# Split fp32r prompt scores and an order from a simulated timeline, in a hybrid attention layer on one Trainium2 core

## The chip, the cores and the metric

The kernel is one program on one NeuronCore of a Trainium2 chip. The metric is the device time of one execution in microseconds (us); lower is better. A core has a matrix engine (TensorE, PE in the profile, its weight loads PEld), three engines for elementwise work (VectorE or DVE, ScalarE or ACT, GpSimd or POOL), and queues that issue DMA transfers, here nearly all on SyncE (SP). Each engine runs its own list of instructions in order and waits for the others by semaphores. Matrix results go to PSUM, eight banks of 128 x 512 f32, and are copied ("evacuated") from there.

## The reference

One layer serves 512 prompt tokens and 64 sample tokens with model width 1024. What matters here, cut to the core:

```python
h = x + W_out [ GDN(n) ; DiffAttn(n) ]     # n = rmsnorm(x), one input projection for both
h = h + MemCrossAttn(rmsnorm(h))
h = h + W2 relu(W1 rmsnorm(h))^2           # then a final rmsnorm

def one(args):                             # differential attention: 4 heads, two halves c of 64 each
    s = jnp.einsum('bqhcd,bkhcd->bhcqk', qi, kf) * scale
    s = jnp.where(visible, s, -jnp.inf)    # whole chunks of 64 keys
    p = jax.nn.softmax(s, axis=-1)
    a = p[:, :, 0] - lam * p[:, :, 1]
    return jnp.einsum('bhqk,bkhe->bqhe', a, vf)

# gated delta (GDN), chunks in sequence, 4 heads: a unit triangular system per chunk, then
def step(S, xs):
    vn = u_c - w_c @ S
    o = qg_c @ S + qk_c @ vn
    S = S * gl_c + kd_c.T @ vn
```

All inputs and outputs are float32. Outputs are the two results, the new keys, values and states.

## The kernel before

Activations stand with features on the partitions and the 576 tokens along the free axis; the 512 prompt tokens are four tiles of 128, the sample a fifth tile (index 4). A projection (`project`) multiplies a 128-column weight block with all tokens in two halves of 256 and 320 tokens. Each f32 weight block is loaded into `raw`, split into a high and a low fp32r part (`wh`, `wl`; L161 on ScalarE, L162 on VectorE) and multiplied with split tokens, so 40 matmuls make one block's projection. Its results go to PSUM tiles `pr` (three banks). The other banks are `ba` (two), `g0`, `g1` and `gs` (one each). In the names of instructions below a tile has a number behind it, one for each time it is taken from its pool.

The gated delta works on chunks c of 128 prompt tokens (0 to 3) and one of the sample (4). `gdn_prep(c, ...)` builds a chunk's triangular system and inverts it level by level: bank g0 for even c, g1 for odd c, tiles `At`, `Dt`, `Y`, `B` with the digit c % 2 (one buffer each for At, Dt and Y) and `X`, `KQ`, `vb`, `kd` (two buffers each). One level is two turns of Y (L113), products with B (L107), a copy of X on ScalarE (L763), Y on VectorE (L764), a product with X, and two subtractions on VectorE (L771, L772). `gdn_scan` then steps the state S in bank gs.

The differential attention goes head by head. `diff_project(h)` makes q, k and v of a head. q is evacuated to `qz` (L957 and `add_to`): two copies of 128 rows, one for each half c, with zeros in the rows of the other half, so that one matmul of 128 rows gives one half's scores. Keys stand turned in `kdT`, a region of the pair tile e5 of all four heads, values in `vtm`, the other half of e5. `diff_head(h, between)` then takes the sample's tile and the four prompt tiles: scores in banks g0 and g1 (f32), maximum (L1019), exponentials (L1022), combination (L1026, L1027), turns, product with the values in bank gs. The cross attention and the feed-forward part follow.

No order is written out by hand for these parts. The functions are called in program order, and a list scheduler of the framework sets, when the kernel is built, in which order each engine gets its instructions, within data dependencies and the number of buffers of each tile. Two places are pinned by hand (`in_order`, `issue_after`).

Of the kernel before, what the change touches and what calls it, by code (L numbers as in the profile page):

```python
# [8 lines left out]
F32 = mybir.dt.float32  # L9
F32R = mybir.dt.float32r  # L10
# [27 lines left out]
def hybrid_layer_kernel(  # L38
# [48 lines left out]
    def view(u, i, a, b):  # L87
        return u[:, i].rearrange("p k t -> p (k t)")[:, : a * b].rearrange("p (a b) -> p a b", a=a)
# [104 lines left out]
    def add_to(dst, b, more):  # L193
        A.copy(dst, more)
        V.tensor_tensor(dst, b, dst, ALU.add)
# [734 lines left out]
    nlam = const([P, 1], "nlam")  # L930
    V.scalar_tensor_tensor(nlam, le[:, 1:2], -LAM0, le[:, 0:1], ALU.add, ALU.subtract)

    od, kdT = e3[:, 0], e5[:, 0]
    vtm = view(e5, 1, 4, 4 * P)
    vs = cp.tile([P, 4, P], F32, tag="vs", name="vs")
    cv2 = view(e3, 1, 4, 4 * P).rearrange("p (i b) n -> p i b n", i=2)
    ckT, cvv = cv2[:, 0].rearrange("p b (c n) -> p (b c) n", n=PAST), cv2[:, 1]

    qz = [cp.tile([P, 2, T], F32, tag=f"qz{i}", name=f"qz{i}") for i in range(2)]
    with tc.issue_after(behind_keys[0]), tc.issue_after(behind_keys[1]):  # L940
        for q2 in qz:
            G.memset(q2[64:, 0, :], 0.0)
            G.memset(q2[:64, 1, :], 0.0)
        G.memset(vs[64:], 0.0)

    def diff_project(h):
        hs = slice(h * P, (h + 1) * P)
        for kind, base in (("q", 2056), ("k", 2568), ("v", 3080)):
            def evac(b, a0, n, more):
                ts_ = slice(a0, a0 + n)  # L950
                if kind == "q":
                    for c in range(2):
                        R = slice(64 * c, 64 * c + 64)
                        if more is not None:
                            add_to(qz[h % 2][R, c, ts_], b[R], more[R])
                        else:
                            (A.copy if c else V.tensor_copy)(qz[h % 2][R, c, ts_], b[R])  # L957
                    return
                d = small("zr", [P, 320])[:, :n] if kind == "v" else kdT[:, h, ts_]
                if more is not None:  # L960
                    add_to(d, b, more)
                else:
                    V.tensor_copy(d, b)
                bt = bank()
                for t in range(2):
                    tr(bt[:, t * P : (t + 1) * P], d[:, t * P : (t + 1) * P])
                if a0:
                    tr(bt[:DEC, 256:384], d[:, 256:])
                src, t2 = bt[:, :256].rearrange("p (t d) -> p t d", t=2), slice(a0 // P, a0 // P + 2)
                if kind == "v":  # L970
                    A.copy(vtm[:, t2, hs], src)
# [11 lines left out]
        nc.sync.dma_start(o_dv_p[0, 0, :, h, :].rearrange("(t p) d -> p t d", p=P), vtm[:, :, hs])  # L983
        nc.sync.dma_start(o_dv_s[0, 0, :, h, :], vs[:DEC, h, :])

    def diff_cache():
# [9 lines left out]
    def diff_head(h, between):  # L996


        hs = slice(h * P, (h + 1) * P)
        so, co = tiny([P, 5], "ta"), tiny([P, 5], "ta")  # L1000
        on = small("an", [P, 5, P])
        for t in (4, 0, 1, 2, 3):
            if t == 1:
                between()
            q0 = QT[t][0]
            nk = q0 + P if t < 4 else PAST + DEC
            nb = (nk + P - 1) // P
            pr = []
            mx, l = tiny([P, 2], "ta"), tiny([P, 2], "ta")
            for c in range(2):  # L1010
                b = bank(f"g{c}")
                qq = qz[h % 2][:, c, q0 : q0 + P]
                if t < 4:
                    mm(b[:, :nk], qq, kdT[:, h, :nk])
                    V.memset(b[:64, nk - 64 : nk], -1e30)
                else:
                    mm(b[:, :PAST], qq, ckT[:, h, :])
                    mm(b[:, PAST:nk], qq, kdT[:, h, SEQ:T])
                V.tensor_reduce(mx[:, c : c + 1], b[:, :nk], AX.X, ALU.max)  # L1019
# [3 lines left out]
                pr.append(p)  # L1023
            V.reciprocal(l, l)
            V.tensor_tensor(l[:, 1:2], l[:, 1:2], nlam, ALU.mult)
            V.tensor_scalar(pr[1][:, :nk], pr[1][:, :nk], l[:, 1:2], None, ALU.mult)  # L1026
            V.scalar_tensor_tensor(pr[0][:, :nk], pr[0][:, :nk], l[:, 0:1], pr[1][:, :nk], ALU.mult, ALU.add)  # L1027
            if nk < nb * P:
                G.memset(pr[0][:, nk : nb * P], 0.0)
            bt = bank()  # L1030
            aT = small("aT", [P, 4, P])
            for kb in range(nb):
                tr(bt[:, kb * P : (kb + 1) * P], pr[0][:, kb * P : (kb + 1) * P])
            A.copy(aT[:, :nb, :], v4(bt, nb))
            po = bank("gs")[:, :P]
            for kb in range(nb):
                if t < 4:
                    vv = vtm[:, kb, hs]
# [584 lines left out]
```

## Time and profile before

| | |
|---|---|
| median of 3 runs | 987.23 us (987.15 to 987.32) |
| profiled execution | 987.2 us |
| its span | 985.5 us, mean granted TensorE clock 0.997 |
| instructions | 16923, of them 6403 matmul records on PE |
| DMA traffic | 90.75 MB, mean 92 GB/s |

The span is the time from the first to the last instruction in the trace of one execution; 1.7 us lie around it. Busy shares add up over the span, so an engine can be busy nearly always and still wait at single places. An f32 matmul leaves two records in the trace, an fp32r matmul or a turn (a matmul with the identity, L113) one. L107 and L113 are the lines of the two helpers `mm` and `tr`, through which all matrix work goes, so groups are told apart by their tiles.

### The profile page before, as it was taken

What the parts mean: (1) busy time and instruction counts of PE and PEld (TensorE: products, weight loads), DVE (VectorE), ACT (ScalarE), POOL (GpSimd) and SP (SyncE); (2) the same over time, 40 slices, a digit from 0 to 9 for tenths busy, and PEclk for the clock granted to TensorE, in tenths of its full rate; (3) what the DMA queues carried; (4) which work ended last, traced back from release to release, by engine and by line L of the source; (5) the groups of instructions that cost most, each with busy time, mean ns of one, the idle gap of its engine ahead of it and who ended that gap; (6) DMA issues with size and microseconds to landing.
All of it is one profiled execution on the core that took longest, in us unless ns stands there. A gap on an engine that the chain in (4) does not pass through costs nothing.

```text
span 985.5 us, 16923 instructions
## 1 busy us (share of the span) xinstructions
PE 968.5 (98%) x6403; PEld 891.2 (90%) x6403; DVE 699.7 (71%) x1570; ACT 530.1 (54%) x1194; POOL 58.8 (6%) x127
## 2 busy tenths in 40 slices
PE   9999999999999999999999999999999999999996
PEld 7989899898888878999999999999999999999996
DVE  6666787877676676666557977657867779978674
ACT  7545575344656665444445657665544445555444
POOL 3341011101000000000000000000000000000000
PEclk9999999999999999999999999999999999999998
DMA  7432340103222647333111414222222223223202
GB/s 212 129 119 65 90 138 23 43 23 103 81 68 68 203 131 227 95 94 99 44 44 58 127 54 127 86 86 86 86 87 86 86 86 86 86 86 86 65 23 96
DMA packets 121714, 90.75 MB, mean 92 GB/s; under 512 B 5564, under 2 KB 112206, under 8 KB 121122
## 3 DMA queue, kind: packets, MB, share of 16 engines
q1 hardware_dynamic: 121266, 89.03, 30.9%
q8 instruction: 50, 0.82, 0.3%
q10 hardware_dynamic: 368, 0.66, 0.2%
q14 instruction: 30, 0.25, 0.1%
HBM read 79.93 MB, written 9.75 MB: 91 GB/s over the span
## 4 chain that ended last, share of the span: by engine, by line
PE 83%; DVE 4%; issue 3%; POOL 2%; DMA 2%; ACT 2%; POOLq 0%; ACTq 0%; SPq 0%; DVEq 0%
PE pr L107 51%; PE g L107 12%; PE ba L107 10%; PE gs L107 6%; PE ba L113 3%; PE g L113 1%; POOL tg L208 1%; DMA r<-in_w_ff_dram 1%; DVE p L457 1%; DVE wl L162 0%; DMA grow<-gdram 0%; DMA raw<-in_w_ff_dram 0%; POOL X L607 0%; POOL X L608 0%; DVE on L809 0%
## 5 line engine op out<-in xcount | busy, mean ns | idle before, releaser
L107 PE MATMUL pr<-u,wh 128*128 128x320 f32 (+2 forms) x1240 | 328.7, 343 | 1.3 <-DVE p L323 1.2
L107 PEld LDWEIGHTS pr<-u,wh 128*128 128x128 f32 x1240 | 212.3, 188 | 18.0 <-DVE p L323 1.8
L107 PE MATMUL pr<-u,wl 128*128 128x256 f32 (+1 forms) x816 | 226.7, 302 | 0.0
L107 PEld LDWEIGHTS pr<-u,wl 128*128 128x128 f32 x816 | 149.9, 189 | 2.7 <-DVE wl L388 0.2
L162 DVE TENSOR_TENSOR wl<-raw,wh 128x1024 fp32r<-128x1024 f32 x65 | 79.4, 1223 | 41.3 <-ACT wh L161 41.0
L161 ACT CAST wh<-raw 128x1024 fp32r<-128x1024 f32 x65 | 68.1, 1048 | 65.7 <-PE pr L107 50.5
L107 PE MATMUL pr<-u,w2h 128*128 128x320 f32 (+1 forms) x384 | 98.5, 340 | 0.0
L1369 ACT CAST w2h<-r 128x512 fp32r<-128x512 f32 x56 | 34.7, 620 | 87.9 <-PE pr L107 85.3
L107 PE MATMUL pr<-f,w2h 128*128 128x320 f32 (+1 forms) x288 | 74.3, 340 | 0.1
L107 PEld LDWEIGHTS pr<-u,w2h 128*128 128x128 f32 x384 | 65.0, 188 | 4.5 <-ACT u L1452 0.3
L107 PE MATMUL pr<-u,w2l 128*128 128x256 f32 (+1 forms) x256 | 65.1, 295 | 0.0
L1454 DVE TENSOR_TENSOR u<-u,pr 128x256 f32<-128x256 f32 x96 | 42.3, 448 | 16.9 <-PE pr L107 16.2
L107 PE MATMUL ba<-u,wl 128*128 128x288 f32 x360 | 53.0, 296 | 0.4 <-ACT keep L1405 0.4
L107 PEld LDWEIGHTS pr<-f,w2h 128*128 128x128 f32 x288 | 48.7, 188 | 4.0 <-issue 1.1
L107 PEld LDWEIGHTS ba<-u,wl 128*128 128x128 f32 x360 | 49.2, 188 | 1.2 <-ACT keep L1405 1.1
L107 PE MATMUL pr<-f,w2l 128*128 128x256 f32 (+1 forms) x192 | 48.8, 295 | 0.0
L107 PEld LDWEIGHTS pr<-u,w2l 128*128 128x128 f32 x256 | 46.9, 188 | 1.5
L208 POOL TENSOR_TENSOR tiny<-tiny,nhalf 128x1 f32<-128x1 f32 (+4 forms) x10 | 8.7, 870 | 631.6 <-DVE tiny L1522 529.8
L1370 DVE TENSOR_TENSOR w2l<-r,w2h 128x512 fp32r<-128x512 f32 x56 | 38.5, 688 | 10.7 <-ACT w2h L1369 10.4
L107 PE MATMUL pr<-wh,u 128*128 128x512 f32 x128 | 41.4, 401 | 0.0
L1414 ACT ACTIVATE c<-c 128x288 f32<-128x288 f32 x48 | 20.6, 443 | 29.5 <-DVE c L1413 29.5
L107 PEld LDWEIGHTS pr<-f,w2l 128*128 128x128 f32 x192 | 35.2, 188 | 1.2
(514 smaller groups left out, 2025.1 us busy)
## 6 DMA issues: line engine op xcount, KB each, us to landing
raw<-in_w_ff_dram SPq DMA_DIRECT2D x36, 512.0 KB
raw<-in_w_in_dram SPq DMA_DIRECT2D x28, 512.0 KB
r<-in_w_ff_dram SPq DMA_DIRECT2D x56, 256.0 KB
raw<-in_w_mem_k_dram SPq DMA_DIRECT2D x8, 512.0 KB
raw<-in_w_mem_v_dram SPq DMA_DIRECT2D x8, 512.0 KB
raw<-in_w_out_dram SPq DMA_DIRECT2D x8, 512.0 KB
raw<-in_w_mem_q_dram SPq DMA_DIRECT2D x8, 512.0 KB
raw<-in_w_mem_o_dram SPq DMA_DIRECT2D x8, 512.0 KB
```

The costliest lines, as they stand in the source:

```text
L107: i = nc.tensor.matmul(out, lhsT, rhs, start=start, stop=stop, skip_group_check=skip_group_check)
L113: i = nc.tensor.transpose(out, in_, ident[:n, :n])
L161: A.copy(wh, raw)
L162: V.tensor_tensor(wl, raw, wh.bitcast(F32), ALU.subtract)
L208: G.tensor_tensor(out, in_, bc(nhalf[: in_.shape[0], 0:1], list(in_.shape)), ALU.pow)
L457: V.scalar_tensor_tensor(yv[:, :n], cb[:, i : i + n], cwt[:, m, i : i + 1], yv[:, :n], ALU.mult, ALU.add)
L1369: A.copy(wh, src)
L1370: V.tensor_tensor(wl, src, wh.bitcast(F32), ALU.subtract)
L1414: A.activation(c, c, AF.Relu)
L1454: V.tensor_tensor(am, am, b, ALU.add)
```

## The change

There are two parts. First, the prompt scores. q and k of the prompt are split into a high and a low fp32r part. q's two parts go to tiles in the tags At0 and At1, and four DMAs stack them for each half c: high part in rows 0 to 63, low part in rows 64 to 127 of `qs`. k's parts go to a pair tile `kdu` (two slots, one for even and one for odd heads, in the place of e5); three DMAs repeat each part in both row halves. A half's scores are then two fp32r matmuls into the same bank, one with the high part of k and one with the low part. The sample's q and new keys go to tiles in the tags Y0 and Y1 and stay f32. Values move from e5 to four tiles in the tags kd, vb, X and KQ, and their output goes by four DMAs instead of one. The halves are taken in the order 1, 0.

Second, the scheduler: `schedule_with_timeline_sim=True` has all instructions of the kernel ordered by a simulation of the whole timeline.

```diff
-    od, kdT = e3[:, 0], e5[:, 0]
-    vtm = view(e5, 1, 4, 4 * P)
+    od = e3[:, 0]
+    kdu = pair(5, F32R)
+    vtm = [small(tag, [P, 4 * P]) for tag in ("kd", "vb", "X", "KQ")]
...
-    qz = [cp.tile([P, 2, T], F32, tag=f"qz{i}", name=f"qz{i}") for i in range(2)]
+    qs = [cp.tile([P, 2, T], F32R, tag=f"qz{i}", name=nm("qs")) for i in range(2)]
+    qy = [small(f"Y{i}", [P, 4 * P]) for i in range(2)]
+    qz, knew = [y[:, : 2 * P].rearrange("p (c n) -> p c n", c=2) for y in qy], [y[:, 2 * P : 2 * P + DEC] for y in qy]
...
+        qn = [small(tag, [P, SEQ], dt=F32R) for tag in ("At0", "At1")]
+        kn = kd_of(h)[:, 0]
...
                 if kind == "q":
-                    for c in range(2):
-                        R = slice(64 * c, 64 * c + 64)
-                        if more is not None:
-                            add_to(qz[h % 2][R, c, ts_], b[R], more[R])
-                        else:
-                            (A.copy if c else V.tensor_copy)(qz[h % 2][R, c, ts_], b[R])
+                    d = b
+                    if more is not None:
+                        d = small("zr", [P, 320])[:, :n]
+                        add_to(d, b, more)
+                    A.copy(qn[0][:, ts_], d[:, :n0])
+                    V.tensor_tensor(qn[1][:, ts_], d[:, :n0], qn[0][:, ts_].bitcast(F32), ALU.subtract)
+                    if a0:
+                        for c in range(2):
+                            R = slice(64 * c, 64 * c + 64)
+                            A.copy(qz[h % 2][R, c, :], d[R, n - P :])
+                            for j in range(2):
+                                nc.sync.dma_start(
+                                    qs[h % 2][64 * j : 64 * j + 64, c, :SEQ].bitcast(F32), qn[j][R].bitcast(F32)
+                                )
                     return
...
+                if kind == "k":
+                    A.copy(kn[:, 0, ts_], d[:, :n0])
+                    V.tensor_tensor(kn[:, 1, ts_], d[:, :n0], kn[:, 0, ts_].bitcast(F32), ALU.subtract)
+                    if a0:
+                        A.copy(knew[h % 2], d[:, 256:])
+                        k0, k1 = (kd_of(h)[:, c, :, :SEQ].bitcast(F32) for c in range(2))
+                        for j in range(2):
+                            nc.sync.dma_start(k1[64 * j : 64 * j + 64], k0[64:])
+                        nc.sync.dma_start(k0[64:], k0[:64])
...
-            for c in range(2):
+            for c in (1, 0):
                 b = bank(f"g{c}")
-                qq = qz[h % 2][:, c, q0 : q0 + P]
                 if t < 4:
-                    mm(b[:, :nk], qq, kdT[:, h, :nk])
+                    for j in range(2):
+                        mm(b[:, :nk], qs[h % 2][:, c, q0 : q0 + P], kd_of(h)[:, c, j, :nk], start=j == 0, stop=j == 1)
...
-    with _tile.TileContext(nc) as tc:
+    with _tile.TileContext(nc, schedule_with_timeline_sim=True) as tc:
```

How it moves instructions is shown at three places. The first is TensorE's list at the first levels of chunks 0 and 1 of the gated delta. Before, with pr_445 the projection of head 0's q, and ba the turns of other tokens:

```order
L113 MATMUL g0_191_1403<-ident_79,Y0_183_1374 128x128 x2
L107 MATMUL g0_191_1403<-Dt0_184_1375,B0_190_1401 128x128 x2
L113 MATMUL g1_228_1550<-ident_79,X_224_1544 128x128
L107 MATMUL pr_445_2585<-u_6_93,wh_443_2581 128x512
L107 MATMUL pr_445_2585<-u_6_93,wl_444_2582 128x256
L107 MATMUL pr_445_2585<-u_6_93,wh_443_2581 128x512
L113 MATMUL ba_249_1655<-ident_79,u_4_78 128x128 x4
L113 MATMUL ba_250_1662<-ident_79,u_4_78 128x128 x4
L107 MATMUL pr_445_2585<-u_6_93,wl_444_2582 128x256
L107 MATMUL pr_445_2585<-u_6_93,wh_443_2581 128x512
L107 MATMUL g0_192_1410<-Y0_183_1374,X_182_1373 128x128 x2
```

After, the same levels:

```order
L113 MATMUL g0_191_1403<-ident_79,Y0_183_1374 128x128 x2
L107 MATMUL g0_191_1403<-Dt0_184_1375,B0_190_1401 128x128 x2
L113 MATMUL g1_233_1574<-ident_79,Y1_225_1545 128x128 x2
L107 MATMUL g1_233_1574<-Dt1_226_1546,B1_232_1572 128x128 x2
L107 MATMUL g0_192_1410<-Y0_183_1374,X_182_1373 128x128 x2
L107 MATMUL g1_234_1581<-Y1_225_1545,X_224_1544 128x128 x2
L113 MATMUL g0_194_1418<-ident_79,Y0_183_1374 128x128 x2
L107 MATMUL g0_194_1418<-Dt0_184_1375,B0_193_1416 128x128 x2
```

The projections that stood between the levels are gone from here; the two chunks' levels alternate directly. No row with pr follows until `pr_476`, 342 matmuls after the last of `pr_473`. The second place is ScalarE's list at the evacuation of head 0's q. Before (qz0 is q's tile, pr_445 its projection; the other rows are steps of chunks 0 and 1):

```order
L757 COPY B0_199_1446<-At0_175_1349 128x256
L194 COPY qz0_2572<-pr_445_2585 64x256
L900 CAST u_149_1257<-ba_253_1675 128x4x128
L194 COPY qz0_2572<-pr_445_2585 64x256
L900 CAST u_149_1257<-ba_254_1682 128x4x128
L770 COPY Y1_225_1545<-Dt1_226_1546 128x32x4
```

After (At0_451 is q's high part, pr_458 the second half of q, zr_463 and zr_467 the halves of k, At0_398 the tile of chunk 4, the last one of the gated delta):

```order
L763 COPY X_406_2425<-g0_418_2462 128x128
L757 COPY B0_423_2484<-At0_398_2403 128x128
L965 CAST At0_451_2586<-zr_457_2611 128x256
L965 CAST At0_451_2586<-pr_458_2616 128x256
L982 CAST u_442_2571<-zr_463_2672 128x256
L194 COPY zr_474_2748<-pr_473_2731 128x256
L982 CAST u_442_2571<-zr_467_2708 128x256
```

q's evacuation stood in the levels of chunks 0 and 1; it now stands behind the last read of chunk 4's At0. The third place is SP's list of DMAs at head 1. Before (raw are weights, out_3 and out_9 the values' outputs):

```order
L983 DMA out_3_dram<-u_4_78 128x4x128
L984 DMA out_9_dram<-vs_2571 64x128
L157 DMA raw_678_3754<-in_w_in_dram 128x8x128
L157 DMA raw_687_3820<-in_w_in_dram 128x8x128
L977 DMA out_2_dram<-p0_531_3037 128x2x128
```

After (qs_448 is head 1's stacked q, u_442 the keys):

```order
L1012 DMA out_9_dram<-vs_2576 64x128
L1207 DMA B0_914_5076<-in_cache_mem_v_dram 128x512
L972 DMA qs_448_2578<-At0_535_2994 64x512 x2
L157 DMA raw_637_3547<-in_w_in_dram 128x8x128
L972 DMA qs_448_2578<-At1_536_2995 64x512 x2
L157 DMA raw_699_3805<-in_w_in_dram 128x8x128
L988 DMA u_442_2571<-u_442_2571 64x2x512 x2
L989 DMA u_442_2571<-u_442_2571 64x2x512
```

Two weight loads now stand between or behind DMAs that wait for head 1's q.

More of the change, by code (lines that the diff above doesn't have):

```diff
@@ L944, in hybrid_layer_kernel, with kd_of @@
         G.memset(vs[64:], 0.0)
+    def kd_of(h):
+        return kdu[:, h % 2].rearrange("p (c j) t -> p c j t", c=2)
     def diff_project(h):
         hs = slice(h * P, (h + 1) * P)
+        qn = [small(tag, [P, SEQ], dt=F32R) for tag in ("At0", "At1")]
+        kn = kd_of(h)[:, 0]
         for kind, base in (("q", 2056), ("k", 2568), ("v", 3080)):
             def evac(b, a0, n, more):
-                ts_ = slice(a0, a0 + n)
+                ts_ = slice(a0, min(a0 + n, SEQ))
+                n0 = ts_.stop - a0
                 if kind == "q":
-                    for c in range(2):
-                        R = slice(64 * c, 64 * c + 64)
-                        if more is not None:
-                            add_to(qz[h % 2][R, c, ts_], b[R], more[R])
-                        else:
-                            (A.copy if c else V.tensor_copy)(qz[h % 2][R, c, ts_], b[R])
+                    d = b
[12 more added lines that the diff above has]
+                                )
                     return
-                d = small("zr", [P, 320])[:, :n] if kind == "v" else kdT[:, h, ts_]
+                d = small("zr", [P, 320])[:, :n]
                 if more is not None:
@@ L970, in evac @@
                 if kind == "v":
-                    A.copy(vtm[:, t2, hs], src)
+                    for t in range(2):
+                        A.copy(vtm[a0 // P + t][:, hs], src[:, t])
                     if a0:
@@ L982, in diff_project @@
             project(weights(w2, base + h * P), xs, evac)
-        nc.sync.dma_start(o_dv_p[0, 0, :, h, :].rearrange("(t p) d -> p t d", p=P), vtm[:, :, hs])
+        for t in range(4):
+            nc.sync.dma_start(o_dv_p[0, 0, t * P : (t + 1) * P, h, :], vtm[t][:, hs])
         nc.sync.dma_start(o_dv_s[0, 0, :, h, :], vs[:DEC, h, :])
@@ L1007, in diff_head @@
             nb = (nk + P - 1) // P
-            pr = []
+            pr = {}
             mx, l = tiny([P, 2], "ta"), tiny([P, 2], "ta")
-            for c in range(2):
+            for c in (1, 0):
                 b = bank(f"g{c}")
-                qq = qz[h % 2][:, c, q0 : q0 + P]
                 if t < 4:
-                    mm(b[:, :nk], qq, kdT[:, h, :nk])
+                    for j in range(2):
+                        mm(b[:, :nk], qs[h % 2][:, c, q0 : q0 + P], kd_of(h)[:, c, j, :nk], start=j == 0, stop=j == 1)
                     V.memset(b[:64, nk - 64 : nk], -1e30)
                 else:
-                    mm(b[:, :PAST], qq, ckT[:, h, :])
-                    mm(b[:, PAST:nk], qq, kdT[:, h, SEQ:T])
+                    mm(b[:, :PAST], qz[h % 2][:, c, :], ckT[:, h, :])
+                    mm(b[:, PAST:nk], qz[h % 2][:, c, :], knew[h % 2])
                 V.tensor_reduce(mx[:, c : c + 1], b[:, :nk], AX.X, ALU.max)
@@ L1022, in diff_head @@
                 A.activation(p[:, :nk], b[:, :nk], AF.Exp, bias=mx[:, c : c + 1], scale=0.125, accum_out=l[:, c : c + 1])
-                pr.append(p)
+                pr[c] = p
             V.reciprocal(l, l)
@@ L1037, in diff_head @@
                 if t < 4:
-                    vv = vtm[:, kb, hs]
+                    vv = vtm[kb][:, hs]
                 else:
```

## The prediction

> **What bounds the kernel now.** I read the page first: the busy shares, the slices, the chain that ended last.
>
> ```profile
> PE 968.5 (98%) x6403; PEld 891.2 (90%) x6403; DVE 699.7 (71%) x1570; ACT 530.1 (54%) x1194; POOL 58.8 (6%) x127
> PE   9999999999999999999999999999999999999996
> PE 83%; DVE 4%; issue 3%; POOL 2%; DMA 2%; ACT 2%; POOLq 0%; ACTq 0%; SPq 0%; DVEq 0%
> ```
>
> TensorE is busy in every slice and carries 83% of the chain. Its waits, asked for next, are short:
>
> ```profile
> PE g L113 <- DVE tg L713: 1.3, 1, 1.3
> PE pr L107 <- DVE p L323: 1.2, 2, 1.0
> ...
> PE pr L113 <- DVE u L233: 0.2, 1, 0.2
> ```
>
> The longest of the twelve rows is 1.3 us. So the time is TensorE's work plus small gaps, and an edit can gain in two ways only: less matrix work, or smaller gaps. It loses wherever TensorE is left without a ready matmul. I therefore looked at the stretches in which latency-bound work (the gated-delta chunks, the attention heads) is mixed with projections, in the view by windows (columns: stretch, length, then busy time of PE, PEld, DVE, ACT and POOL, granted clock, DMA share, GB/s):
>
> ```profile
> 121.00:250.00 129.00, 125.89 (x963) 116.08 (x961) 101.27 (x269) 67.91 (x160) 15.30 (x18) 1.00 0.25 70
> 135.00:240.00 105.00, 102.75 (x804) 95.41 (x803) 81.72 (x213) 50.20 (x124) 10.82 (x14) 1.00 0.17 43
> 252.00:332.00 80.00, 79.06 (x486) 67.24 (x485) 53.55 (x183) 47.46 (x160) 3.28 (x5) 1.00 0.27 79
> ```
>
> The second row is the gated-delta part from the first turned X of chunks 0 and 1 to the fourth level of chunk 4. The same window, asked for tile pr alone, shows what fills it:
>
> ```profile
> 135.00:240.00 105.00, 49.65 (x230) 34.57 (x229) 5.68 (x13) 4.45 (x14) 1.00 0.17 43
> ```
>
> Of TensorE's 102.75 us, 49.65 are projections (the q, k, v of heads 0 and 1), laid between the small matmuls of the chunks. Without them the chunks keep TensorE busy for 53.1 us of 105.
>
> **The scores.** The prompt scores are f32 matmuls now (rows of the groups by form; columns: busy, mean ns of one, idle before; an f32 matmul leaves two records).
>
> ```profile
> L107 PE MATMUL pr<-wh,u 128*128 128x512 f32 x128 | 41.4, 401 | 0.0
> L107 PE MATMUL g<-u,qz 128*128 128x256 f32 x32 | 9.4, 394 | 0.0
> L107 PE MATMUL g<-u,qz 128*128 128x512 f32 x16 | 8.4, 609 | 0.0
> L107 PE MATMUL g<-u,ql 128*128 128x256 f32 x24 | 7.5, 313 | 0.0
> L107 PE MATMUL g<-u,qz 128*128 128x384 f32 x16 | 7.0, 519 | 0.0
> L107 PE MATMUL g<-u,qz 128*128 128x128 f32 x16 | 3.4, 295 | 0.1
> ```
>
> Half of the 32 records at 256 columns are the sample's and stay f32, so the prompt's are 8.4 + 7.0 + 4.7 + 3.4 = 23.5 us busy for 32 matmuls, eight of each width. After, each is two fp32r passes. A pass of 512 columns is 41.4/128 = 0.32 us by the first row; by columns 384 take 0.24; for 256 I take 0.20, between half the first row (0.16) and 7.5/24 = 0.31 in the row of ql; 128 columns of fp32r are not in this trace, between a quarter of the first row (0.08) and a record of the f32 form, 3.4/16 = 0.21, and I take 0.15. Sixteen of each: 16 x 0.91 = 14.6 us. That saves about 9; some of these busy times overlap neighbours, so I take 8, and 4 to 12 as the bounds (12 if every record of the pair halves its cost, 4 if the narrow passes win nothing).
>
> For the width of 512 the Trainium skill ("TensorE: Matmul & The Clock Gate", "Back-to-back issue gap") gives an isolated gap of N / 2.4 + 2.5 ns, 216 ns; by it all four widths would need 8.7 us, an estimate from that page, the saving would be 15 and the total 7 us lower. The row's 0.32 us, with weight loads in it, speaks against this here.
>
> **What the scores add elsewhere.** Per head, q and k are each split into a high part (ScalarE cast, twice) and a low part (VectorE subtract, twice), k's new copies included some ten more instructions of 0.4 us, against four 64-row copies saved: about +3 us per head over two engines that the page shows at 71% and 54%. Four more table loads on ScalarE stand in the new order. I put these at 0 on the end as long as projections are queued on TensorE. Where none is, they are in the stretches priced below. The 40 added DMAs on SP are sized by these rows (chain of waits and timeline):
>
> ```profile
> 118.45 1.24 DMA gdram<-p
> 119.77 4.02 DMA grow<-gdram
> 165.58 1.28 ACT L701 ACT_TABLE_LOAD   x1
> ```
>
> A stacking DMA is bounded by 1.2 and 4.0 us; k needs two in a row (L988, then L989 into what L988 read), 2.5 to 8 us. For head 0 three projections' worth of matmuls stand between k's evacuation and its first prompt score, some 20 us, which covers it. On SP the weight loads of later projections are queued behind q's stacking (the third place shown in the change): `raw_637` and `raw_699` now wait until head 1's q is evacuated. They serve head 2's v and head 3's q (`pr_640`, `pr_702`), some 40 us of TensorE work after head 1's q (`pr_542`); I take 0, and 8 us if this cover is gone.
>
> **The order of the gated-delta stretch.** This is the big term. In the new order of TensorE no projection stands between the last matmul of `pr_473` (first half of head 0's v) and `pr_476` (its second half). In between stand 342 small matmuls: all levels of chunks 0 and 1, four scans, chunks 2 and 3 and four levels of chunk 4. The tie is in the buffers: q's parts now sit in the tags At0 and At1 with one buffer each, so ScalarE's cast into At0_451 stands behind the last read of chunk 4's At0_398 (second place shown), q's banks pr and the zr copies stay held until then, and no bank is left for a projection. Before, q went to its own tile and k to a region of its own.
>
> TensorE's work in there, at issue distances from these timeline rows (columns: start, length):
>
> ```profile
> 143.30 1.04 PE L113 MATMUL ba<-ident,u 128*128 128x128 f32 x8
> 163.38 1.05 PE L107 MATMUL gs<-vb,X 128*128 128x128 f32 x8
> 164.94 0.60 PE L113 MATMUL g<-ident,u 128*128 128x128 f32 x4
> ```
>
> Four more transposes take 1.04 - 0.60 = 0.44, 0.11 each. An f32 matmul is two records: (1.05 - 0.61)/2 = 0.22, with the 0.61 of the next fence. So 180 x 0.22 + 128 x 0.11 + 34 half-size or wide ones at about 0.15 = 59 us; with the 53.1 from before beside it I take 60.
>
> How long does the chunks' chain need when nothing else runs? One level of one stream, from the timeline:
>
> ```profile
> 142.16 0.61 PE L107 MATMUL g<-Dt,B 128*128 128x128 f32 x4
> 145.19 0.62 PE L107 MATMUL g<-Dt,B 128*128 128x128 f32 x4
> 145.29 0.28 DVE L771 TENSOR_TENSOR Y<-Dt,g 128x128 f32<-128x128 f32 x1
> 146.09 0.41 DVE L772 TENSOR_TENSOR Dt<-Dt,g 128x256 f32<-128x256 f32 x1
> 146.41 0.41 DVE L764 SCALAR_TENSOR_TENSOR Y<-lev,g 128x256 f32<-128x256 f32 x1
> 146.95 0.38 PE L113 MATMUL g<-ident,Y 128*128 128x128 f32 x2
> 147.17 0.61 PE L107 MATMUL g<-Dt,B 128*128 128x128 f32 x4
> 147.62 0.61 PE L107 MATMUL g<-Y,X 128*128 128x128 f32 x4
> ```
>
> In a row: 0.38 + 0.61 + 0.41 + 0.61 + 0.28 + 0.41 = 2.7 us, whereas two streams together need 2 x (2 x 0.11 + 4 x 0.22) = 2.2 us of TensorE. So even at its ideal TensorE idles in each level; before, a level of one stream took 147.17 - 142.16 = 5.0 us behind the projections. The whole stretch is bounded below by VectorE: the new order has 192 VectorE instructions from `vb_178` to the split of q's second half; at the mean of the window, 81.72/213 = 0.384 us, 74 us. It is bounded above by the 105 us that the same chain took with projections in its way. I take 84, nearer the lower end since the projections that stretched it are gone, but not at it, since VectorE stood idle for 22% of the window before. TensorE then idles 84 - 60 = 24 us (14 to 45). The old gaps of the window 121 to 250, 129 - 125.89 = 3 us, go with it: +21 net. These projections are not lost work: they are done afterwards, when nothing latency-bound is left to be hidden under them.
>
> **The heads.** In the new order two stretches have prompt scores, turns and values of a head with no projection between: head 0's tiles 1 to 3 (from `gs_497` to `pr_625`) and head 1's (from `ba_583` to `pr_704`), about 8 us of TensorE each; a third, in head 2, is thinner. A prompt tile of 512 keys needs on VectorE two reductions and more:
>
> ```profile
> 267.57 0.40 DVE L1026 TENSOR_SCALAR p<-p,ta 128x384 f32<-128x384 f32 x1
> 267.89 0.68 DVE L1019 TENSOR_REDUCE ta<-g 128x1 f32<-128x512 f32 x1
> 268.49 0.60 DVE L1027 SCALAR_TENSOR_TENSOR p<-p,ta,p 128x384 f32<-128x384 f32 x1
> ```
>
> That is 2 x 0.68 + 0.4 + 0.6 and about 0.7 of small ones, 3.1 us; three tiles and the new splits of k make 10 to 11 us against 8, plus the last tile's way through ScalarE. I take 3.5 us for each of the two (0.5 to 7): +7. The feed-forward part is ordered differently too, but it stays full of projections: 0, and 3 either way.
>
> **The sum.** It is made on the profiled execution: 987.2 us, of which 985.5 are the span and 1.7 lie around it; the median of the runs is 987.23, the same. 987.2 - 8 (scores) + 21 (gated-delta stretch) + 7 (heads) = 1007. Low ends together: 987.2 - 12 + 11 + 1 = 987; high ends: 987.2 - 4 + 42 + 14 = 1039.
>
> **The rivals.** (A) The simulated timeline fits the chip: the small matmuls are ready when TensorE comes to them. Then the stretch costs about 3 us of idle time, the heads none: 987.2 - 8 - 3 + 3 = 979. It decides from the point where the stretch runs below 71 us, as then the idle is under the 8 + 3 saved. For it: rows of VectorE overlap a little at issue, so 74 is no hard floor. Against: 2.7 us per level against 2.2. Chance 0.13. (B) The chain runs near VectorE's floor of 74 to 76: +11 to +13 and heads +3: 992, with the scores at their best 988. Chance 0.14. (C) The chunks keep the 105 us, because their own chain and not the projections set it: +42 and heads +14 at most: 1035 or so. VectorE's idle 22% speaks for it, the 5.0 us of a level against 2.7 against it. Chance 0.08. (D) SP's queue: a weight load behind q's stacking comes late, in heads 1 to 3 once each up to 8 us: 1007 + 8 to 24, 1019. Chance 0.05. (E) The granted clock falls in the thin stretch. At the end of the span TensorE is busy for about half of a window and the clock is below 1:
>
> ```profile
> 975.00:980.00 5.00, 2.63 (x23) 2.23 (x21) 2.13 (x5) 2.30 (x4) 0.85 (x1) 0.92 0.00 0
> ```
>
> In the new stretch it would be busy 60/84 = 71%, in pauses of one or two us. If the clock halved there, its 60 us would become up to 120, longer than the 84: +36, 1043. Chance 0.02. The Trainium skill ("TensorE: Matmul & The Clock Gate", "A second HAM failure mode: psum-queue depth-cycling") tells of such throttling from frequent short idling; the 1.00 in the three windows above neither bears this out nor excludes it.
>
> **How the numbers follow.** The forecast case, with the stretch between 77 and 98 us, has 0.58. Its 1007 is the prediction. The range 986 to 1028 leaves out A below and most of C and E above. 0.2% (2 us) is about what a measurement of this kernel can tell from no change. Faster: A and a little of B, 0.15. Same: 0.05, from B. Slower: 0.80.
>
> **What would show it.** In the profile after, the window from the first turned X of chunk 0 to `pr_476` should be 77 to 98 us long with TensorE busy 60 to 75% and tile pr absent; the waits of PE on DVE and ACT at tiles Y, X, Dt should sum to over 15 us instead of under 1; the page's PE share should fall to 95 or 96%; two short stretches of idle should follow between 270 and 320 us. The rows of g<-u,qs should sum to 10 to 16 us. A stretch of about 70 us with TensorE over 85% busy would prove me wrong.

## The result: 1042.9 us, 5.6% slower

| | before | after |
|---|---|---|
| median | 987.28 us (987.15 to 987.56, 4 runs) | 1042.93 us (1040.03 to 1044.77, 4 runs) |
| ratio to before | 1 | 1.0561 (1.0535 to 1.0586) |
| profiled span | 985.5 us | 1038.3 us |
| mean granted clock | 0.997 | 0.976 |

The profiled run is the fastest of the four after, 2.9 us under their median. The sign was right; the size was not. 1007 us was forecast with a range up to 1028. The page of the kernel after, in the rows that were shown of the one before:

```profile
PE 979.1 (94%) x6403; PEld 906.4 (87%) x6403; DVE 703.6 (68%) x1578; ACT 544.1 (52%) x1226; POOL 58.6 (6%) x127
PE   7999998777889899999999899999999999999996
...
PEclk9899999989798999999999999999999999999999
...
PE 83%; DVE 7%; ACT 4%; DMA 2%; issue 2%; SPq 1%; POOL 0%; POOLq 0%; DVEq 0%; ACTq 0%
```

TensorE is less than 90% busy in ten of the 40 slices, where before it was in the last alone: the first, six from 156 to 311 us, one from 337 to 363 us, one from 571 to 597 us and the last. The granted clock is below 0.9 in four slices (one from 26 to 52 us, three between 208 and 337 us), where before it was only in the last. The chain carries more of VectorE and ScalarE (11% instead of 6%). The five longest of TensorE's waits, by their sums:

```profile
PE pr L107 <- ACT kd L410: 7.2, 1, 7.2
PE g L107 <- ACT p L1050: 6.2, 9, 1.3
PE g L113 <- DVE Y L751: 4.1, 3, 2.1
PE g L107 <- DVE Y L764: 3.8, 9, 1.7
PE g L113 <- DVE Dt L772: 3.4, 4, 1.8
```

The three rows at the bottom are the levels of the gated delta, the second is the score matmuls of the attention heads, which wait for ScalarE's exponentials. The first was not in my forecast at all: one wait of 7.2 us. By windows (same columns as in the prediction), with tile pr alone in the second fence:

```profile
17.50:34.00 16.50, 9.27 (x58) 8.69 (x58) 7.00 (x10) 4.69 (x13) 2.10 (x6) 0.69 0.46 109
...
165.90:271.80 105.90, 80.36 (x558) 67.83 (x556) 70.48 (x196) 39.43 (x103) 9.92 (x13) 0.91 0.07 22
...
305.00:323.00 18.00, 13.42 (x64) 10.51 (x63) 10.48 (x42) 9.49 (x40) 0.00 (x0) 0.81 0.20 51
```

```profile
165.00:272.00 107.00, 1.29 (x8) 0.97 (x7) 1.31 (x3) 0.74 (x2) 0.91 0.07 22
```

The stretch without projections runs from the first turned X of chunk 0 (165.9 us) to `pr_476` (271.8 us): 105.9 us, about the 105 us of the window before with 49.65 us of projections in it. To compare the same work, take the stretch from the first turned X to one and the same matmul, the product with X in the third level of chunk 4. Tile pr in it, in the kernel before, in scores only (an experiment below) and in the kernel after:

```profile
135.10:240.50 105.40, 49.94 (x231) 34.64 (x229) 5.68 (x13) 4.35 (x13) 1.00 0.17 44
```

```profile
134.30:233.70 99.40, 26.14 (x120) 17.89 (x118) 1.26 (x3) 1.80 (x7) 1.00 0.11 28
```

```profile
165.90:270.20 104.30, 0.17 (x1) 0.00 (x0) 0.19 (x1) 0.37 (x1) 0.91 0.06 20
```

It took 105.4 us with 50 us of projections in it, 99.4 with 26 and 104.3 with next to none. The parts of it differ. Up to the last product of scan 3 (the last small `ba<-vn,kd`) the kernel after needs 92.6 us where the one before needs 102.7. From there to the end it needs 11.7 us instead of 2.7, as in the simulated order all of chunk 4's levels come behind scan 3, where before two of them were done by then. That the sum is about 105 us again is in part chance.

The next table accounts for the whole difference. From each trace I took the start of every matmul and subtracted the distance that the same form has back to back at full clock (about 0.11 us for a turn, 0.23 for f32 and 0.11 for fp32r at 128 columns, 0.23 for fp32r at 512, and so on). What is left is time in which TensorE stood still, or what a lower clock added. The stages are cut by the amount of matrix work done so far, so the parts of a stage differ a little where the order differs. About 9.5 us of each span lie ahead of the first and behind the last matmul. The rows depend on the distances chosen (the -0.8 shows by how much), their differences between kernels hardly. In us:

| stage (matrix work done, us) | before | after | simulated order only | scores only | scores, free buffers |
|---|---|---|---|---|---|
| start (0 to 25) | 6.0 | 15.6 | 16.7 | 6.2 | 6.2 |
| first projections (25 to 146) | 4.0 | 2.9 | 1.7 | 3.1 | 3.2 |
| gated delta (146 to 240) | 4.7 | 44.6 | 29.7 | 21.6 | 3.8 |
| attention heads (240 to 320) | 2.6 | 17.7 | 22.0 | 3.9 | 3.7 |
| cross attention (320 to 590) | 4.3 | 7.5 | 20.5 | 4.4 | 7.1 |
| feed-forward (590 to end) | 4.8 | -0.8 | 0.0 | 6.3 | 4.5 |
| matrix work | 949.6 | 941.3 | 949.6 | 941.3 | 941.3 |

Between the first two columns: -8.3 for the scores, +9.6 at the start, -1.1, +39.9 in the gated delta, +15.1 in the heads, +3.2, -5.6: +52.8, the difference of the profiled spans. The medians differ by 55.7.

### The profile page after: what moved, and what is told of

Read it like the earlier page. It is cut to its first block, busy times and chain, and to the rows that moved or that the text cites. A ratio compares the mean times of both kernels' runs of the same rounds, so it can differ in the third digit from the quotient of the medians.

```text
span 1038.3 us, 17028 instructions
## 1 busy us (share of the span) xinstructions
PE 979.1 (94%) x6403; PEld 906.4 (87%) x6403; DVE 703.6 (68%) x1578; ACT 544.1 (52%) x1226; POOL 58.6 (6%) x127
## 4 chain that ended last, share of the span: by engine, by line
PE 83%; DVE 7%; ACT 4%; DMA 2%; issue 2%; SPq 1%; POOL 0%; POOLq 0%; DVEq 0%; ACTq 0%
PE pr L107 53%; PE ba L107 11%; PE g L107 10%; PE gs L107 6%; PE ba L113 2%; PE g L113 2%; DMA raw<-in_w_in_dram 1%; DMA grow<-gdram 1%; ACT p L1050 1%; DVE ta L1047 1%; DVE Y L764 0%; SPq L129 0%; ACT X L763 0%; DVE At L705 0%; DMA dtb<-in_a_log_dram 0%
## 5 line engine op out<-in xcount | busy, mean ns | idle before, releaser
L107 PE MATMUL pr<-u,wh 128*128 128x320 f32 (+2 forms) x1240 | 320.5, 340 | 0.8 <-DVE u L1161 0.3
L107 PE MATMUL pr<-u,wl 128*128 128x256 f32 (+1 forms) x816 | 223.4, 298 | 0.0
L107 PE MATMUL pr<-u,w2l 128*128 128x320 f32 (+1 forms) x256 | 65.4, 295 | 0.0
L107 PE MATMUL pr<-wh,u 128*128 128x512 f32 x128 | 38.7, 396 | 0.0
L1159 DVE TENSOR_TENSOR u<-u,pr 128x256 f32<-128x256 f32 (+1 forms) x48 | 21.5, 450 | 18.1 <-PE pr L107 18.0
```

What stands on the lines that cost most here:

```text
L107: i = nc.tensor.matmul(out, lhsT, rhs, start=start, stop=stop, skip_group_check=skip_group_check)
L1159: V.tensor_tensor(hm, hm, b, ALU.add)
```

## The experiments

Each ran beside the kernel before on the same chip; ratios are to it, with their 95% intervals.

**The two halves of the change.** One flag and one diff undo either half.

```diff
 # simulated order only: the kernel before
-    with _tile.TileContext(nc) as tc:
+    with _tile.TileContext(nc, schedule_with_timeline_sim=True) as tc:
 # scores only: the kernel after
-    with _tile.TileContext(nc, schedule_with_timeline_sim=True) as tc:
+    with _tile.TileContext(nc) as tc:
```

> The kernel before with the order of the simulated timeline, the scores left as they were. Its order has 52 us of small matmuls without a projection from g0_186 to pr_603, since the projections of heads 0 and 1 are all put ahead of the gated-delta levels, and the Exp of a_log stands ahead of the first weight splits on ScalarE. If the simulated order is what costs the time: start +8 to +10 us, gated-delta stretch +30 to +40, heads +5, feed-forward -5, together 1022 to 1040 us. If the buffers in At0 and At1 are what costs it: within 10 us of before, 980 to 997 us.

> The split scores with the scheduler of before. Its order has 31 us of small matmuls without a projection, before pr_476. If the simulated order is what costs the time: -8 for the scores and +10 to +15 for that stretch, 985 to 998 us, and no wait at the start. If the buffers cost it: the stretch idles 20 us and more, heads +5, above 1010 us.

Measured: simulated order only 1051.18 us, 1.0643 (1.0627 to 1.0658); scores only 999.20 us, 1.0123 (1.0100 to 1.0145). The order costs 64 us by itself, more than the 1022 to 1040 us that I allowed; by the table these are 25 in the gated delta, 19 in the heads, 16 in the cross attention and 11 at the start, less 7 elsewhere. The scores by themselves cost 12 us instead of saving 8, a little above the range of 985 to 998. Under the simulated order they do save: 1051.18 to 1042.93 is 8.3 us. The simulated order without any new buffer, in the profile, with tile pr alone in the third fence:

```profile
PE pr L107 <- ACT kd L410: 7.6, 1, 7.6
```

```profile
168.20:282.10 113.90, 93.45 (x686) 83.12 (x684) 69.19 (x184) 40.27 (x99) 8.76 (x11) 0.97 0.11 31
```

```profile
168.20:282.10 113.90, 24.99 (x145) 21.48 (x144) 3.22 (x8) 1.90 (x5) 0.97 0.11 31
```

The wait at the start is about the same, and the gated delta starts at 168.2 us here too instead of 135.1. In this order nearly all projections of head 0 stand ahead of it and those of head 1 ahead of scan 0: the 25 us of pr lie in the first 29 us of this window, and the 84.6 us from 197.5 to 282.1 have none. So the late start and most of the empty stretch (84.6 of 106 us) need no new buffer: qz, kdT and vtm are where they were before.

**The tie of q to At0 and At1.** This was the reason that my forecast gave for the stretch.

```diff
-        qn = [small(tag, [P, SEQ], dt=F32R) for tag in ("At0", "At1")]
+        qn = [small("aT", [P, SEQ], dt=F32R) for _ in range(2)]
```

> The changed kernel with q's two parts in the two buffers of tag aT instead of At0 and At1. If the tie of q to At0 is what took the projections out of the gated-delta stretch, it returns 15 us or more: below 1028 us. If the simulated order and the other ties do it: 1035 to 1048 us, with tile pr absent from a stretch of about 100 us as in the changed kernel.

Measured: 1056.02 us, 1.0697 (1.0669 to 1.0726), 13 us slower than the changed kernel and above both ranges. The tags aT belong to the heads, and TensorE now waits 5.1 us there in a row that has 0.6 in the changed kernel, and 3.3 us for a stacking DMA:

```profile
PE gs L107 <- ACT aT L1062: 5.1, 9, 1.5
...
PE g L107 <- DMA u<-u: 3.3, 1, 3.3
```

Tile pr is still absent from 170.3 to 275.1 us. The tie to At0 did not empty the stretch under the simulated order; my reason falls.

**All ties, with the scheduler of before.** Here q is first copied to od's free slot, k to kdT and v to vtm (both in e5, as before), the sample's q to a tile of its own (that of odd heads to the tag Y1), and the parts are split from these copies.

```diff
-    od = e3[:, 0]
-    kdu = pair(5, F32R)
-    vtm = [small(tag, [P, 4 * P]) for tag in ("kd", "vb", "X", "KQ")]
+    od, kdT = e3[:, 0], e5[:, 0]
+    vtm = view(e5, 1, 4, 4 * P)
...
+        parts[h] = kp = [[small(next(tags), [P, SEQ], dt=F32R) for j in range(2)] for c in range(2)]
...
+                    A.copy(od[:, h, a0 : a0 + n], b)
+                    q = od[:, h, :SEQ]
+                    A.copy(qn[0], q)
+                    V.tensor_tensor(qn[1], q, qn[0].bitcast(F32), ALU.subtract)
...
+                d = small("zr", [P, 320])[:, :n] if kind == "v" else kdT[:, h, a0 : a0 + n]
...
```

> The split scores with the scheduler of before, and no buffer shared with the gated delta before the projections are evacuated: q goes to od's free slot, k to kdT and v to vtm as before, the sample's q to a tile of its own, and the split parts are made from these copies (q's in the tags aT, k's in kd, vb, X and KQ). TensorE's order has projections in the gated-delta stretch as in the kernel before. If the ties of the buffers made the scores slow (999.2 us with this scheduler): the 8 us of the scores come out, 977 to 984 us. If the splits and stacking DMAs themselves cost it: 990 us and more.

Measured: 981.04 us, 0.9941 (0.9928 to 0.9954). This is faster than both kernels, by 6.4 us than the one before. The table has 8.3 us of matrix work saved, so the splits and the stacking DMAs (six per head for k here) cost at most about 2 us; what had made the scores slow was where their results were put, and with it how they were evacuated. Tile pr between 165 and 240 us, in the kernel before, scores only, and free buffers, in this order:

```profile
165.00:240.00 75.00, 33.37 (x155) 23.53 (x156) 3.94 (x9) 2.28 (x6) 1.00 0.15 39
```

```profile
165.00:240.00 75.00, 11.08 (x49) 7.90 (x50) 1.33 (x3) 0.74 (x2) 0.98 0.11 29
```

```profile
165.00:240.00 75.00, 35.44 (x164) 24.80 (x164) 3.13 (x7) 1.92 (x5) 1.00 0.17 45
```

33 us of projections stood there before, 11 with the new buffers, 35 with free ones.

An earlier attempt untied q alone (parts in aT, the sample's q and keys in a tile of their own) and left k in kdu and v in the gated delta's tags.

```diff
-    qy = [small(f"Y{i}", [P, 4 * P]) for i in range(2)]
+    qy = cp.tile([P, 4 * DEC], F32, tag="qy", name="qy")
...
-        qn = [small(tag, [P, SEQ], dt=F32R) for tag in ("At0", "At1")]
+        qn = [small("aT", [P, SEQ], dt=F32R) for _ in range(2)]
...
```

> The scores-only kernel with q alone untied: its parts in the tags aT, the sample's q and new keys in a tile of their own; k and v stay in their new places. Its order has a stretch of 25 us of small matmuls without a projection instead of 31. If the ties add up: 992 to 998 us, between 999.2 and the kernel with all of them gone. If q's tie is the one that counts: below 988 us.

Measured: 1006.56 us, 1.0196 (1.0181 to 1.0210), a miss: not better than scores only, but 7 us worse, though pr is busy for 17.45 us from 165 to 240 us instead of 11.08. So the ties do not add up one by one; that the other ties still hold the same banks would explain it but is not shown. Which of k's or v's counts most was not tried alone.

**The same free buffers in the simulated order.**

> The scores with free buffers (981.0 us with the scheduler of before) in the simulated order. Its order has 44 us of small matmuls without a projection before pr_640. If the simulated order alone loses the time, whatever the buffers: 1036 to 1050 us, 8 us under the simulated order with the f32 scores (1051.2). If order and buffers lose it together: below 1025 us.

Measured: 1058.70 us, 1.0728 (1.0712 to 1.0744). The two theories expected below 1025 or 1036 to 1050; it is above both. So the order loses time whatever the buffers: 64 us with the f32 scores, 44 with the new buffers (999.20 to 1042.93), 78 with the free ones (981.04 to 1058.70).

**The start.** ScalarE in the kernel after:

```profile
17.08 0.59 ACT L288 CAST u<-g 128x512 fp32r<-128x512 f32 x1 [0.24 <-PE g L113]
25.50 0.20 ACT L515 ACTIVATE tiny<-dtb 128x4 f32<-128x4 f32 x1 [7.83 <-DMA dtb<-in_a_log_dram]
...
26.82 1.16 ACT L410 CAST kd<-raw 128x512 fp32r<-128x512 f32 x2
```

A tiny exponential of a_log (L515) stands ahead of a weight split (L410), and its operand's DMA, issued at 21.76 us, lands at about 25.5. Everything behind it on ScalarE waits for 7.83 us. Before, the split came at 19.03 us and L515 at 29.06.

```diff
+    V.scalar_tensor_tensor(dtb[:, 1, :], ab[:, 0, 0:4], 0.0, dtb[:, 1, :], ALU.mult, ALU.add)
     A.activation(ea, dtb[:, 1, :], AF.Exp)
```

> The changed kernel with the Exp of a_log made to read a value that is there only later (one more VectorE instruction adds zero times it), so that ScalarE no longer waits for the small DMA of a_log ahead of the first weight splits. If that wait is the whole loss of the start: 8 to 10 us less than the changed kernel, 1033 to 1036 us, and PE's wait on L410 gone. If the weights themselves are late: no change.

Measured: 1032.13 us, 1.0447 (1.0432 to 1.0463): 10.8 us less than the changed kernel. PE's wait for L410 is gone, and the first turned X comes at 156.4 us instead of 165.9, 9.5 earlier. This is more than the 7.2 us of the wait. The likely rest is the clock: in the changed kernel it was at half from 23.0 to 33.2 us (0.69 on average in the window above), in this run it stayed at 1.00 there.

**Is the stretch set by TensorE, by its clock, or by the chain?** Useless matmuls are queued behind 34 groups of the stretch.

```diff
...
+            while a0 and fill:
+                after = last_of[fill.pop(0)]
+                for _ in range(4):
+                    mm(b[:, 384:], ones, ones)
+                    tc.add_manual_dep(
+                        nc.cur_bb.bb.instructions[-1], after,
...
```

> The changed kernel with 136 useless f32 matmuls of 128 columns (constants into free columns of the bank pr_458, 0.22 us each, 30 us in all) placed on TensorE behind 34 groups of the gated-delta stretch. If the stretch is set by latency and the halved clock adds to it: the clock stays at 1.00 from 200 to 275 us, the added work costs nothing, 1030 to 1041 us. If the clock costs nothing: 1043 to 1055 us. If TensorE itself bounds the stretch: 1065 us and more.

Measured: 1045.93 us, 1.0589 (1.0572 to 1.0606). The stretch, and tile pr (the added matmuls) in it:

```profile
166.30:275.20 108.90, 99.62 (x827) 91.45 (x826) 69.63 (x190) 38.32 (x101) 9.88 (x13) 1.00 0.07 22
```

```profile
166.30:275.20 108.90, 35.51 (x273) 32.68 (x273) 0.49 (x1) 0.00 (x0) 1.00 0.07 22
```

TensorE took 35.51 us more in the stretch, and it grew by 3 us only, 105.9 to 108.9 (by 7.3 us, 104.3 to 111.6, to the same matmul of chunk 4). So the amount of TensorE's work does not bound it; a chain of steps that wait for each other does. In the changed kernel this chain, followed back from the end, lies for 46 of the 105.9 us on TensorE's own small matmuls, for 36 on VectorE and for 12 on ScalarE.

The granted clock went from 0.91 to 1.00, and the stretch did not get shorter; the total lies in the range that I gave for "the clock costs nothing". This does not show that it cost nothing, as the added matmuls stand in the chain's way and can hide what the full clock gains. In the changed kernel TensorE was busy for 16.2 of the 20.2 us of the stretch that had the half clock:

```profile
210.70:214.20 3.50, 3.44 (x17) 3.04 (x17) 2.93 (x9) 2.10 (x5) 0.86 (x2) 0.51 0.00 0
221.00:227.80 6.80, 6.15 (x27) 5.71 (x28) 3.07 (x8) 2.35 (x7) 0.00 (x0) 0.50 0.00 0
261.90:271.80 9.90, 6.64 (x24) 4.87 (x22) 8.31 (x23) 5.45 (x15) 0.42 (x1) 0.50 0.27 80
```

The chain lies on TensorE for 10.2 of these us, so an estimate of the clock's cost in the stretch is 5 us at most, half of that.

**Are the late steps ahead of the levels to blame?** Three runs changed what stands there.

The first one, on the kernel before in the simulated order, holds the projections of heads 0 and 1 behind given chunk matmuls:

```diff
...
+            if (kind, h) in GATES:
+                tc.add_manual_dep(
+                    next(i for i in nc.cur_bb.bb.instructions[at:] if i.engine == mybir.EngineType.PE),
+                    first_of[GATES[kind, h]],
...
```

The second, on the changed kernel, holds each SiLU of z behind the exponentials of chunks 0 and 1 on ScalarE (`behind_exp` adds that order to the instruction just made); the third leaves the SiLU out:

```diff
                 A.activation(z, b[:, :256], AF.Silu)
+                behind_exp()
...
```

```diff
-                A.activation(z, b[:, :256], AF.Silu)
+                A.copy(z, b[:, :256])
...
```

> The kernel before with the simulated order, and on TensorE alone six added orders: the q, k and v projections of heads 0 and 1 may not start ahead of a given gated-delta matmul (about where they stood before). If the simulated order loses because it uses up the projections before the chunks' levels begin: the gated-delta stretch gains 25 us or more, 1010 to 1027 us. If it loses by how it orders VectorE and ScalarE in the chunks: above 1035 us.

> The changed kernel with one more order on ScalarE alone: no SiLU of the gate z ahead of the exponentials L701 of chunks 0 and 1 (they stand at 138.8 us and 151.2 us there, with four SiLU groups and their tables between). In its order the levels then begin two projections earlier on TensorE. If the late exponential makes the levels start late and the lateness is carried to the end: g0_186 at 150 to 158 us instead of 165.9, and 8 to 14 us less, 1029 to 1035 us. If the stretch behind keeps its length and only moves: the same start, but 1038 to 1043 us.

> The changed kernel with the SiLU of the gate z left out (copied instead), so that ScalarE loads 5 tables instead of 15 and changes none between the two exponentials of chunks 0 and 1; the order of the instructions stays the same. If the table loads make the chunks' levels start late: g0_186 at 157 to 160 us instead of 165.9, and 1032 to 1038 us in all. If only the order of ScalarE and VectorE does it: 1040 to 1044 us.

Measured: gated 1059.36 us, 1.0729 (1.0714 to 1.0744); exponential first 1041.11 us, 1.0549 (1.0530 to 1.0568); no SiLU tables 1037.56 us, 1.0518 (1.0500 to 1.0535).

The gated order put the projections back between the levels, as its window and its tile pr show:

```profile
161.50:300.00 138.50, 121.90 (x847) 110.42 (x848) 79.32 (x202) 46.62 (x111) 9.70 (x12) 0.94 0.14 36
```

```profile
161.50:300.00 138.50, 53.35 (x296) 45.42 (x296) 6.20 (x14) 3.81 (x10) 0.94 0.14 36
```

53 us of projections are there, about as many as before, and yet it got 8 us slower than the simulated order alone. The first turned X comes at 161.5 us although no projection of the heads stands ahead of it, and the gated delta then ends at 317.7 us (`g0_426`; 307.4 without the gates, 248.0 before). The expectation that the loss is only a matter of projections used up too early falls with this run. It is not a clean test, though: the gates keep the projections away ahead of the levels too, and TensorE is busy for 9.46 of the 19.2 us from 142.3 to 161.5.

With the exponential first the levels do start earlier, 157.4 instead of 165.9 us, as expected, but scan 0 comes at 191.6 instead of 188.5 us and the end 0.5 us earlier by the profile: the second of the two ranges. The third run's total lies in the range for "the loads make the levels start late", but the levels start at 163.2 us there and not at 157 to 160. Without the table loads the whole chain moves by 2.7 us, and the profiled span is 2.8 us shorter; the medians differ by 5.4, of which the spread of both kernels (3 to 5 us) may be part. So the loads are a small part, and the start of the levels by itself is none.

## Why the prediction was wrong

- **The gated-delta stretch, +21: the step that failed.** Its place and kind were right (1.29 us of pr at its two ends in 107 us, TensorE 76% busy); its length was not. I bounded it by VectorE's 74 us and by the 105 us of before, and took 84, "nearer the lower end since the projections that stretched it are gone". They had stretched it little. With the scheduler of before and about half of them the same work took 99.4 us instead of 105.4. In the simulated order without them, chunks 0 to 3 alone took 92.6 us up to the end of scan 3 instead of 102.7, and the levels of chunk 4 came on top. Of all rivals C, to which I gave 0.08, comes nearest: its +42 stands against +39.9 in the table. It has the length right and the reason in the main; that the length came out at 105 again is in part chance. The 5.0 us of a level and VectorE's 78% could not tell a long chain from a stretched one, as TensorE was busy for 102.75 of the 105 us there. The levels of chunks 0 and 1, from the first turned X to the first turned Dt, took 23.1 us before and 18.7 after, so the projections had stretched them by about a quarter, where I had set the 5.0 us of a level against a sum of 2.7.
- **The reason for the stretch.** I named the tie of q to At0 and At1. Moving q did not take it away, and the simulated order has most of the stretch (84.6 us) without any new buffer. The ties are real, but they show with the other scheduler: where the parts and copies stand costs 18 us there (981.04 to 999.20). Untying q alone did not help (1006.56), so k's or v's place must have a part in it, which the forecast did not price.
- **The start, taken as nothing: +9.6.** The forecast went by the order of TensorE in the middle and left out ScalarE's first rows, where L515 stands. Moving that one row gained 10.8 us.
- **The heads, +7: measured +15.1.** The mechanism was right (the waits are on p L1050 and on VectorE), the term too small: the first such stretch alone, 305 to 323 us, leaves 4.6 us idle at a clock of 0.81, and TensorE's scores wait nine times on ScalarE's exponentials (6.2 us), where I had priced VectorE and only the last tile's way through ScalarE.
- **The scores, -8: right.** 949.6 to 941.3 us of matrix work, and 6.4 us of the whole time with free buffers. That the two kernels in the simulated order differ by 8.3 us too is chance, as their idle times differ stage by stage (29.7 to 44.6 in the gated delta, 20.5 to 7.5 in the cross attention). The passes:

```profile
L107 PE MATMUL g<-u,qs 128*128 128x512 f32 x16 | 5.7, 437 | 1.9 <-ACT p L1050 1.8
L107 PE MATMUL g<-u,qs 128*128 128x384 f32 x16 | 4.0, 363 | 0.1
L107 PE MATMUL g<-u,qs 128*128 128x128 f32 x16 | 3.0, 271 | 0.3 <-ACT p L1050 0.3
L107 PE MATMUL g<-u,qs 128*128 128x256 f32 x16 | 2.9, 293 | 1.0 <-ACT p L1050 1.0
```

15.6 us busy where I had 14.6. The estimate from the Trainium skill ("TensorE: Matmul & The Clock Gate", "Back-to-back issue gap") was 8.7 us. It counts from start to start, where busy times of neighbours overlap, so the busy rows that I set against it cannot decide: passes of 512 columns that ran back to back started 0.23 us apart in this trace, near its 0.216, and all four widths come to about 10 us by such distances.

- **The feed-forward part, 0 with 3 either way: -5.6.** The simulated order is better there: no gap at all is left, against 4.8 us before.
- **SP's queue (D): no sign of it.** None of PE's listed waits is for a weight load.
- **The clock (E): it fell, and cost less than I priced.** I had 36 us for a halved clock in the whole stretch; it was halved for 20 of the 106 us, 5 us at most by the estimate above. That E's 1043 is the measured time is chance.
- **The signs.** TensorE's waits at Y, X and Dt sum to 12.3 us, under the 15 that I named, and its busy share is 94%, under 95. The stretch was 8 us longer than the 98 that I allowed. B's 992 is a slip: its own terms, -8, +11 to +13 and +3, give 993 to 995.

What stays open: how long the chunks' chain is with the scheduler of before and no projection at all in it, which no run had; and which instructions of VectorE and ScalarE in the simulated order lengthen the way through the chunks once projections stand between the levels. To the same matmul of chunk 4 it took 104.3 us there with none, 132.9 with 223 records of pr between (simulated order only) and 149.9 with 336 (gated), where the scheduler of before hid 229 of them in 105.4. Three single changes to them moved the end by 0.5 us, 2.8 us, and the wrong way; the two engines' whole order against the order of before was not tried alone.

## What to carry to other kernels

A chain that is hidden by other work has a length of its own, and a window in which the covering engine is busy all the time does not show it. Do not put it near its lower bound without a run that has less cover: half of the projections gone took 6 of 105 us off here. The length belongs to one order, too; in the simulated order projections between the levels did lengthen it. When a change reorders everything, read the first rows of every engine: a tiny instruction that waited for a DMA held ScalarE's queue for 7.83 us here. And a buffer that is shared with an unrelated stage is an order in disguise: evacuate to a place that is free early, and split or restack from there (981.0 us against 999.2 with the same arithmetic and the same scheduler).

## What the runs showed of the hardware

In the changed kernel the granted clock fell to half in spells of 3.4 to 13.7 us, in or just behind stretches where TensorE's stream was broken by waits, the longest 7.2 us and the others under 3. The mean clock was 0.69 between 17.5 and 34 us, 0.91 in the stretch and 0.81 in the first head; with the stretch filled by useless matmuls it stayed at 1.00. The Trainium skill ("TensorE: Matmul & The Clock Gate", "A second HAM failure mode: psum-queue depth-cycling") tells of such throttling by frequent short idling; the traces agree that it occurs. What it cost here stays an estimate, 5 us at most in the stretch, as the filled run had the full clock and was no shorter.
